# Pages of a paged cache fetched by GpSimd's row gathers instead of plain transfers, in a hybrid decoder step

## The chip, the cores and the metric

The kernel runs on one core of a Trainium2 chip. The engines are PE (TensorE, matrix products), DVE (VectorE), ACT (ScalarE), POOL (GpSimd) and SP (SyncE, which only issues transfers here). Each has its own queue, works it off in order, and waits for others by semaphores. The metric is the device time of one execution in microseconds (us), the median of several runs.

## The reference, cut to what matters

One step of two layers is computed for a prompt of 512 rows and for 8 samples with one new row each. The part that the change touches is the attention of the samples (NSA, native sparse attention), whose keys and values lie in paged caches in HBM: 128 rows a page, 8 pages a sample, and a page table that says which physical page each is.

```python
    s_c = jnp.einsum('btghd,bngd->btghn', qg, kc, preferred_element_type=f32)
...
    p_c = masked_softmax(s_c, m_c)
    o_c = jnp.einsum('btghn,bngd->btghd', p_c, vc.astype(f32))
...
    imp = jnp.einsum('btghn,nj->btgj', p_c, overlap_matrix(kc.shape[1], n_slc))
...
    _, idx = lax.top_k(score, topn)
...
    s_s = jnp.einsum('btghd,bgtnld->btghnl', qg, sel[..., 0, :], preferred_element_type=f32)
...
    o_s = jnp.einsum('btghnl,bgtnld->btghd', p_s, sel[..., 1, :].astype(f32))
...
    o = g[..., 0:1] * o_c + g[..., 1:2] * o_s + g[..., 2:3] * o_w
```

Here `kc`, `vc` are all rows of the compressed cache behind a small MLP, `sel` the 16 blocks of 64 rows that `imp` ranks highest, and `o_w` the same attention on a window of 512 rows.

With 1024 cached rows a sample has 16 whole blocks and its own new row, so nearly all pages of the selected cache are used, and the kernel loads them all and masks. There are three kinds of pages, 64 of each: of the compressed cache (`c_cmp`, 128 rows by 256 floats, 128 KB), of the selected keys (`c_sk`, 128 by 128, 64 KB) and of the selected values (`c_sv`, 64 KB). The window's keys and values (`c_wk`, `c_wv`) aren't paged.

## The kernel before, in words

Every dense product is made in three matmuls of split operands (`mm3`, L309 to L313), since a float32 is held as a high and a low part. Such a tile covers 128 output channels by 520 rows in two halves, x0 (256 columns) and x1 (264), 24 matmuls each.

The first stage (to about 285 us) makes q, k, v from the input (`wh_q`, `wh_k`, `wh_v`), rotates them, and runs the samples' compress and key products between those tiles, in the order of the list `ORDER` (L70): `q`, `k` are dense tiles, `c0` to `c7` are `compress(b)` of sample b, `r0` to `r5` are `scores_of`, `p` is a preparation, `d` the gates, `n` a normalisation. Behind the list come the 40 `xz` tiles (L990), whose matmuls the scheduler spreads to fill PE's idle time. They write one buffer `u`, whose last 11 columns POOL copies out (`sstg<-u`, L1002), then `uc`, then `uth`. Attention of the prompt follows, from about 285 to 690 us (`sc` the scores, L1110; `po` the value products, L1186; `ptl`, `pth` the split parts of its softmax; `QS` its scaled and split queries), with the xz tiles in its gaps. In it the samples' value products run too: 12 steps of `nsa_sample_out` (L1598) with a tile `vt` each, of which the first 8 take paged values. `st`, `Cb`, `Bm`, `xs`, `cum` are loads of the state-space part, which is prepared then.

`gather` (L804) fetches one page. SP reads its number out of the table `pti` ([1, 64], loaded at L741) into a register, and a plain transfer with an address that depends on it follows on SP (its lines stand in the diff below).

`compress(b)` (L923) fetches 8 pages into a tile `cc` and multiplies it in 32 matmuls (`cmpAB`, L934). `scores_of` (L1494) fetches 16 pages into a tile `kt` for r0 to r3 and makes the products `scS` (L1491); for r4 and r5 it takes `c_wk` in one plain transfer of 1 MB. `cc` and `kt` share three buffers (tag `big`), so that a gather waits until the tile that is three allocations earlier is used up. `vt` has two buffers. All weights (`raw_...`, L301) also come over SP's queue.

The Tile scheduler sets the order of every engine: it simulates a timeline with costs of its own and puts the instructions of each engine in the order that this gives. So an edit at one place can move instructions at many others.

Of the kernel before, what the change touches and what calls it, by code (L numbers as in the profile page):

```python
# [11 lines left out]
F32 = mybir.dt.float32  # L12
F32R = mybir.dt.float32r
I32 = mybir.dt.int32
BF16 = mybir.dt.bfloat16
AF = mybir.ActivationFunctionType
ALU = mybir.AluOpType
# [13 lines left out]
NPHYS = 80  # L31
# [226 lines left out]
def step_kernel(ctx: ExitStack, tc: tile.TileContext, I, O):  # L258
    nc = tc.nc
# [12 lines left out]
    def V(name, j=0):  # L272
        o, n = VEC[name]
        return vec[:, o + j:o + j + 1]
# [65 lines left out]
    def rstd(wk, ps, scale, name, last=None, out=None):  # L340
        n = ps.shape[-1]
        if last is not None:
            last = table(last)
        l = wk.tile([128, 266], F32, tag="lnv", name="lnv", bufs=1)
        r = wk.tile([128, 266], F32, tag="rs", name=name, bufs=2)[:, :n] if out is None else out
        with tc.issue_after(last.ins) if last is not None else ExitStack():
            nc.scalar.activation(l[:, :n], ps, AF.Ln, bias=epsT, scale=scale)
            done_["exp"] = nc.scalar.activation(r, l[:, :n], AF.Exp, scale=-0.5)
        return r
# [332 lines left out]
    def mixer(begin):  # L682
# [7 lines left out]
        def gen(n=512, name="gen"):  # L690
            return mp.tile([128, 512], F32, tag="g", name=name, bufs=3)[:, :n]
# [20 lines left out]
        ap = ax.enter_context(tc.tile_pool(name="ma", bufs=1))  # L712
# [4 lines left out]
        vcS = ap.tile([64, NB, 128], F32, name="vcS")  # L717
        vnew = ap.tile([64, 128], F32, name="vnew")
        pnT = ap.tile([64, 128], F32, name="pnT")
        pti = ap.tile([1, 64], I32, name="pti")  # L720
        u_ = ap.tile([128, T], F32, name="u")
        uc = ap.tile([128, T], F32, name="uc")
        hp = ap.tile([128, 24, NB], F32, name="shp")
# [6 lines left out]
        tp = p1.enter_context(tc.tile_pool(name="mt", bufs=2))  # L730
        x = []
        for hf in range(2):
            x.append(tp.tile([128, KD, 266], F32, tag="big", bufs=BIG, name="x"))
            n = HALF[hf][1] - X0[hf]
# [3 lines left out]
                wq = [wload(I["w_in"][0], 1, "k", "u")[0]]  # L738
        alr = tp.tile([128, 32], F32, name="alr", bufs=1)
        rsm = tp.tile([128, T], F32, name="rsm", bufs=1)  # L740
        nc.sync.dma_start(pti, I["pt"])  # L741
        c0_, c1_ = CST["cos"][0], CST["maskc"][0]
        cst = tp.tile([128, c1_ - c0_], F32, name="cst", bufs=1)

# [11 lines left out]
        def behind_x(hf, ins):  # L756

            with tc.issue_after(ins):
                if hf == 0:
                    nc.scalar.dma_start(cst, I["cst"][:, c0_:c1_])  # L760
                    nc.scalar.dma_start(vec[:, 64:], I["vec"][:, 64:])
                    return
                nc.scalar.dma_start(w2, I["w2"])
                nc.scalar.dma_start(alr, I["alr"].to_broadcast([128, 32]))
                nc.scalar.dma_start(b2v, I["b2v"].to_broadcast([64, 128]))
                nc.scalar.dma_start(pe.rearrange("p a b c -> p (a b c)"), I["pe"])
                for kv in range(2):
                    nc.scalar.dma_start(w1[kv].rearrange("p a b -> p (a b)"), I["w1"][kv])

        for hf, (c0, c1) in enumerate(HALF):  # L770
            ps = gen(c1 - c0, "ns")
            o, e = c0 - X0[hf], c1 - X0[hf]
            xh, xl = x_in[hf]
            for k in range(KD):
                sq = P["bk"].tile([128, 266], F32, tag="sq", name="sq", bufs=SQB)[:, :c1 - c0]
                last = nc.scalar.activation(sq, x[hf][:, k, o:e], AF.Square)
                if hf == 0 and k == 0:
                    behind_x(0, last.ins)
                nc.tensor.matmul(ps, ones, sq, start=k == 0, stop=k == KD - 1)
                if hf:  # L780
                    nc.vector.tensor_scalar(xh[:, k], x[hf][:, k, 0:e], V("ng", k), None, op0=ALU.mult)
                else:
                    nc.scalar.activation(xh[:, k], x[hf][:, k, 0:e], AF.Copy, scale=V("ng", k))
                nc.vector.scalar_tensor_tensor(xl[:, k], x[hf][:, k, 0:e], V("ng", k), xh[:, k].bitcast(F32), op0=ALU.mult,
                                               op1=ALU.subtract)
            rstd(P["bk"], ps, 1.0 / D, "rs1", None, rsm[:, c0:c1])
# [15 lines left out]
                split(xh[:, k], xl[:, k], xf)  # L802

        def gather(dst, src, n):  # L804

            page = nc.values_load(pti[0:1, n:n + 1], engines=(mybir.EngineType.SP,), min_val=0, max_val=NPHYS - 1,
                                  skip_runtime_bounds_check_because="the table holds numbers of the cache's pages")
            nc.sync.dma_start(dst, src.rearrange("(n p) c -> n p c", p=128)[bass.ds(page, 1)].rearrange("n p c -> p (n c)"))

        def dense2(mt, name):  # L810
            w = wq.pop() if wq else wload(I["w_in"][mt], 1, name, "u")[0]
# [66 lines left out]
        for kv in range(2):  # L878
# [25 lines left out]
            else:  # L904
                for g in range(2):
# [3 lines left out]
                                               op1=ALU.add)  # L909
# [13 lines left out]
        def compress(b):  # L923
            ccb = tp.tile([128, 8, 256], F32, tag="big", bufs=BIG, name="cc")
            for n in range(8):
                gather(ccb[:, n], I["c_cmp"], b * 8 + n)
            cv = ccb.rearrange("p n (v g j c) -> p v j g n c", v=2, g=2, j=8)
            for kv in range(2):
                hid = tp.tile([128, 2, 64], F32, tag="chs", name="chs", bufs=2)
                nc.vector.memset(hid[:, :, 63:64], 0.0)  # L930
                psa = gen(256, "cmpAB").rearrange("p (a g n) -> p a g n", a=2, g=2)
                for a in range(2):
                    for j in range(8):
                        nc.tensor.matmul(psa[:, a].rearrange("p g (n c) -> p g n c", c=8), w1[kv][:, a * 8 + j],  # L934
                                         cv[:, kv, j], start=j == 0, stop=j == 7)
                ub = tp.tile([128, 2, 64], F32, tag="ub", name="ub", bufs=2)
                nc.scalar.activation(ub, psa[:, 1], AF.Identity, bias=bias[:, kv:kv + 1])
                nc.vector.tensor_add(hid[:, :, 0:63], psa[:, 0, :, 0:63], ub[:, :, 1:64])
                th = tp.tile([128, 2, 64], F32, tag="cts", name="cts", bufs=2)
                nc.scalar.activation(th, hid, AF.Tanh, scale=0.5)  # L940
                nc.vector.scalar_tensor_tensor(hid, th, 1.0, hid, op0=ALU.add, op1=ALU.mult)
                ps = gen(128, "kvcS")
                if kv == 0:
                    nc.tensor.matmul(ps, w2[:, 0:128], hid.rearrange("p g c -> p (g c)"), start=True, stop=True)
                    for g in range(2):
                        sl = slice(g * 64, g * 64 + 64)
                        nc.scalar.activation(kcS[sl, b], ps[sl, g * 64:g * 64 + 64], AF.Identity,
                                             bias=V("cb2", 0)[sl], scale=0.5)
                else:
                    for g in range(2):  # L950
                        nc.tensor.matmul(ps[0:64, g * 64:g * 64 + 64], hid[:, g], w2[:, 128:192], start=True, stop=True)
                    nc.vector.scalar_tensor_tensor(vcS[:, b], ps[0:64], 0.5, b2v, op0=ALU.mult, op1=ALU.add)

        prep, scores_of, softmaxes = nsa_sample(mp, gen, C, tp, knew, qs, kcS, PT, pnT, gS, gather)
        dtg = tp.tile([128, T], F32, name="dtg", bufs=1)

# [5 lines left out]
        for op in ORDER.split():  # L962
            n = int(op[1:])
# [61 lines left out]
        for c in range(5):  # L1025
            n = 128 if c < 4 else NB
# [45 lines left out]
        tp = bp.enter_context(tc.tile_pool(name="mb", bufs=2))  # L1072
# [146 lines left out]
        def state_rows(tp, g, q=nc.sync):  # L1219
# [6 lines left out]
            for t in range(4):  # L1226
                for n in range(2):
# [7 lines left out]
                    yield  # L1235

        sample, sample_end = nsa_sample_out(gen, tp, first, PT, pnT, vcS, vnew, gather, d_yn)
        rows_of = itertools.chain(*(state_rows(tp, g, nc.gpsimd) for g in range(HG)))
        for hg in range(4):
# [15 lines left out]
        tp = sp_.enter_context(tc.tile_pool(name="ms", bufs=1))  # L1255
# [397 lines left out]
    with tc.tile_pool(name="wum", bufs=3, side="right") as P["wu"]:  # L1653
        new = mixer(begin)()
# [30 lines left out]
```

## Time and profile before

| | us |
|---|---|
| median of 3 runs (1977.76 to 1982.85) | 1979.02 |
| the profiled execution | 1979.54 |
| its span, first to last instruction | 1977.8 |
| PE busy | 1824.6 (92%) |
| DVE busy | 1427.8 (72%) |
| ACT busy | 969.3 (49%) |
| POOL busy | 181.6 (9%) |

The mean granted clock of PE is 0.964 of full speed. "Busy" of an engine leaves out the issuing of transfers on SP. A wait is put down to the producer that ended last. The chain of work that ended last holds PE for 67% of its length, DVE for 12% and transfers for 6%.

### The profile page before, as it was taken

To read this page: it belongs to the slowest core of one execution; us is meant where nothing else is said; L and a number is where in the kernel's file an instruction comes from. 1 tells how busy PE (TensorE), PEld (TensorE's weight loads), DVE (VectorE), ACT (ScalarE), POOL (GpSimd) and SP (SyncE) were. 2 spreads that over 40 slices of the span, in tenths; PEclk is the share of its full clock that TensorE was granted. 3 is DMA by queue.
4 is the path that set the end of the run, shared out by engine and by line. 5 is a ranking of instruction groups with operands and counts; after the bars stand their busy time and mean duration, and the time that the engine had idled before them with its cause. 6 is when DMAs were issued, how large, how long until landed. Compare 5 with 4: busy or idle time off the path is not lost.

```text
span 1977.8 us, 37956 instructions
## 1 busy us (share of the span) xinstructions
PE 1824.6 (92%) x14411; PEld 1706.2 (86%) x14411; DVE 1427.8 (72%) x3404; ACT 969.3 (49%) x2083; POOL 181.6 (9%) x226
## 2 busy tenths in 40 slices
PE   6998869899899889999899999997998989999997
PEld 5997868788788788988899999996766889999997
DVE  5764759788788698978767776575787765666766
ACT  3223436566467577656555433344126755444433
POOL 0000011010000003130000111000100000000100
PEclk9999989899899989999999999998998999999999
DMA  8446254253331385434245433221453223434421
GB/s 288 120 137 189 76 157 147 79 168 101 114 99 60 90 287 168 143 132 126 75 144 164 133 107 109 86 72 47 104 143 108 86 75 118 123 118 123 144 65 49
DMA packets 125947, 240.90 MB, mean 122 GB/s; under 512 B 16499, under 2 KB 63236, under 8 KB 125444
## 3 DMA queue, kind: packets, MB, share of 16 engines
q1 hardware_dynamic: 120676, 221.45, 36.6%
q0 software_dynamic: 4000, 13.73, 2.3%
q10 hardware_dynamic: 1088, 3.29, 0.4%
q8 instruction: 114, 1.87, 0.4%
q14 instruction: 69, 0.57, 0.1%
HBM read 200.75 MB, written 30.88 MB: 117 GB/s over the span
## 4 chain that ended last, share of the span: by engine, by line
PE 67%; DVE 12%; DMA 6%; ACT 6%; SPq 5%; issue 3%; POOL 1%; ACTq 0%; DVEq 0%; POOLq 0%
PE up L311 8%; PE up L312 8%; PE up L313 8%; PE acc L311 5%; PE acc L312 5%; PE acc L313 5%; PE dn L311 4%; PE dn L312 4%; PE dn L313 4%; SPq L607 3%; PE cmpAB L934 2%; PE pT L1173 1%; PE yd L1359 1%; PE po L1187 1%; DVE wl_xz L293 1%
## 5 line engine op out<-in xcount | busy, mean ns | idle before, releaser
L311 PE MATMUL dn<-gh,wh_dn 128*128 128x256 f32 (+1 forms) x704 | 198.0, 285 | 4.2 <-ACT gh L462 2.6
L313 PE MATMUL dn<-gh,wl_dn 128*128 128x256 f32 (+1 forms) x704 | 199.1, 284 | 0.0
L312 PE MATMUL dn<-gl,wh_dn 128*128 128x256 f32 (+1 forms) x704 | 198.8, 283 | 0.0
L450 DVE SCALAR_TENSOR_TENSOR c<-up,vec,c 128x511 f32<-128x511 f32 (+2 forms) x216 | 139.1, 646 | 14.6 <-ACT c L447 14.2
L311 PEld LDWEIGHTS dn<-gh,wh_dn 128*128 128x128 f32 x704 | 131.9, 189 | 5.6 <-ACT gh L462 2.9
L312 PEld LDWEIGHTS dn<-gl,wh_dn 128*128 128x128 f32 x704 | 133.4, 189 | 0.4 <-POOL gl L463 0.2
L313 PEld LDWEIGHTS dn<-gh,wl_dn 128*128 128x128 f32 x704 | 133.0, 189 | 0.0
L463 POOL TENSOR_TENSOR gl<-gm,gh 128x520 fp32r<-128x520 f32 (+2 forms) x54 | 61.8, 1144 | 703.5 <-ACT gh L462 703.4
L445 DVE TENSOR_TENSOR up<-up,rsx 128x520 f32<-128x520 f32 (+2 forms) x108 | 65.0, 604 | 81.3 <-PE up L313 79.8
L477 DVE TENSOR_TENSOR facc<-dn,facc 128x256 f32<-128x256 f32 (+1 forms) x160 | 66.4, 425 | 67.0 <-PE dn L313 66.6
L292 ACT ACTIVATE wh_up<-raw_up 128x1024 fp32r<-128x1024 f32 x68 | 72.0, 1059 | 72.7 <-PE up L312 47.2
L311 PE MATMUL acc<-x0hm,wh_xz 128*128 128x256 f32 x320 | 98.1, 307 | 6.0 <-ACT uc L999 3.7
L293 DVE TENSOR_TENSOR wl_up<-raw_up,wh_up 128x1024 fp32r<-128x1024 f32 x68 | 83.3, 1225 | 23.6 <-ACT wh_up L292 23.4
L312 PE MATMUL acc<-x0lm,wh_xz 128*128 128x256 f32 x320 | 95.1, 297 | 0.0
L313 PE MATMUL acc<-x0hm,wl_xz 128*128 128x256 f32 x320 | 94.9, 296 | 0.0
L311 PE MATMUL acc<-x1hm,wh_xz 128*128 128x264 f32 x320 | 93.4, 292 | 0.8 <-ACT u L997 0.8
L312 PE MATMUL acc<-x1lm,wh_xz 128*128 128x264 f32 x320 | 92.9, 290 | 0.0
L313 PE MATMUL acc<-x1hm,wl_xz 128*128 128x264 f32 x320 | 92.7, 290 | 0.0
L447 ACT ACTIVATE c<-up,vec 128x520 f32<-128x520 f32 (+2 forms) x108 | 74.8, 694 | 33.4 <-DVE up L445 32.7
L292 ACT ACTIVATE wh_dn<-raw_dn 128x1024 fp32r<-128x1024 f32 (+1 forms) x48 | 47.5, 989 | 88.2 <-PE dn L312 62.3
L293 DVE TENSOR_TENSOR ptl<-pT,pth 128x512 fp32r<-128x512 f32 (+1 forms) x96 | 65.1, 685 | 33.7 <-ACT pth L292 33.5
L292 ACT ACTIVATE pth<-pT 128x512 fp32r<-128x512 f32 (+1 forms) x96 | 56.3, 596 | 58.0 <-PE pT L1173 54.5
(583 smaller groups left out, 6857.4 us busy)
## 6 DMA issues: line engine op xcount, KB each, us to landing
raw_up<-in_w_up SPq DMA_DIRECT2D x68, 512.0 KB, 3.7
raw_xz<-in_w_in SPq DMA_DIRECT2D x40, 512.0 KB, 3.8
raw_dn<-in_w_down SPq DMA_DIRECT2D x32, 512.0 KB, 3.9
raw_wo<-in_w_out SPq DMA_DIRECT2D x24, 512.0 KB, 3.8
raw_pw<-in_w_pw SPq DMA_DIRECT2D x24, 512.0 KB, 4.0
spill<-uth SPq DMA_DIRECT2D x40, 260.0 KB, 2.5
st<-in_st SPq DMA_DIRECT2D x40, 256.0 KB, 3.0
cc<-in_c_cmp SPq DMA_DIRECT2D x64, 128.0 KB, 2.5
```

The lines of the kernel that those rows point to most:

```text
L292: nc.scalar.activation(hi, src, AF.Copy)
L293: (eng or nc.vector).tensor_sub(lo, src, hi.bitcast(F32))
L311: nc.tensor.matmul(ps, hi[:, wc], xh, start=first, stop=False)
L312: nc.tensor.matmul(ps, hi[:, wc], xl, start=False, stop=False)
L313: nc.tensor.matmul(ps, lo[:, wc], xh, start=False, stop=last)
L445: nc.vector.tensor_mul(u(a, e0), u(a, e0), rv[:, a:e0])
L447: nc.scalar.activation(c[:, rs], u(r0, r1), AF.Identity, bias=V("fb", l * 44 + mt), scale=W(2, mt))
L450: nc.vector.scalar_tensor_tensor(c[:, a:e], u(a - d, e - d), W(2 - d, mt), c[:, a:e], op0=ALU.mult, op1=ALU.add)
L463: nc.gpsimd.tensor_sub(gl[:, rs], gm[:, rs], gh[:, rs].bitcast(F32))
L477: nc.vector.tensor_add(f, ps, f)
L607: nc.sync.dma_start(x4[m][j * 32:j * 32 + 32, i, a:b], glu[m][i * 32:i * 32 + 32, 1 + j + a:1 + j + b])
L934: nc.tensor.matmul(psa[:, a].rearrange("p g (n c) -> p g n c", c=8), w1[kv][:, a * 8 + j], cv[:, kv, j], start=j == 0, stop=j == 7)
```

## The change

`gather` becomes one indirect transfer on POOL's queue: for each of the 128 partitions it fetches the row of the cache whose number stands in column n of a table `idx`, [128, 64]. To make that table, the page table is loaded into all 128 partitions (a broadcast transfer), an IOTA on POOL writes each partition's number, and two DVE operations compute page × 128 + partition. The reads of `pti` into SP's registers and the 192 transfers on SP are gone; `c_wk` and `c_wv` stay plain transfers on SP. The bytes and the buffers are the same. Lines behind L775 are 5 later in the changed kernel.

```diff
-        pti = ap.tile([1, 64], I32, name="pti")
+        idx = ap.tile([128, 64], I32, name="idx")
...
-        nc.sync.dma_start(pti, I["pt"])
+        pti = tp.tile([128, 64], I32, name="pti", bufs=1)
+        nc.sync.dma_start(pti, I["pt"][0:1, :].to_broadcast([128, 64]))
...
+        ptf = tp.tile([128, 2, 64], F32, tag="qz", name="ptf")
+        nc.gpsimd.iota(ptf[:, 0], pattern=[[0, 64]], base=0, channel_multiplier=1,
+                       allow_small_or_imprecise_dtypes=True)
+        nc.vector.tensor_copy(ptf[:, 1], pti)
+        nc.vector.scalar_tensor_tensor(idx, ptf[:, 1], 128.0, ptf[:, 0], op0=ALU.mult, op1=ALU.add)
...
         def gather(dst, src, n):
-
-            page = nc.values_load(pti[0:1, n:n + 1], engines=(mybir.EngineType.SP,), min_val=0, max_val=NPHYS - 1,
-                                  skip_runtime_bounds_check_because="the table holds numbers of the cache's pages")
-            nc.sync.dma_start(dst, src.rearrange("(n p) c -> n p c", p=128)[bass.ds(page, 1)].rearrange("n p c -> p (n c)"))
+            nc.gpsimd.indirect_dma_start(out=dst, out_offset=None, in_=src,
+                                         in_offset=bass.IndirectOffsetOnAxis(ap=idx[:, n:n + 1], axis=0))
```

The scheduler makes another order of this. On POOL, the place between the copies of old state at its start (`o_...`) and the first copy of u, before:

```order
L543 DMA o_ch<-in_h_cf 16x15360
L417 DMA o_fh<-in_h_ff 16x5632
L986 ISA
L986 TENSOR_TENSOR shist<-shist,vec 128x576
L1002 COPY sstg<-u 128x11 x5
L1085 MEMSET masks 128x384
```

and now:

```order
L417 DMA o_fh<-in_h_ff 16x5632
L812 DMA cc<-in_c_cmp,idx 128x256 x32
L812 DMA kt<-in_c_sk,idx 128x128 x32
L812 DMA cc<-in_c_cmp,idx 128x256 x8
L812 DMA kt<-in_c_sk,idx 128x128 x16
L812 DMA cc<-in_c_cmp,idx 128x256 x8
L812 DMA kt<-in_c_sk,idx 128x128 x16
L812 DMA cc<-in_c_cmp,idx 128x256 x16
L1007 COPY sstg<-u 128x11
L991 TENSOR_TENSOR shist<-shist,vec 128x576
L1007 COPY sstg<-u 128x11 x5
```

All 128 gathers of `cc` and `kt` stand there in one queue: c0 to c3, r0 and r1, c4, r2, c5, r3, c6 and c7.

On POOL in attention, behind the loads of the state (`st`, numbered by buffer), before:

```order
L1230 DMA st_6315<-in_st 128x512
L1230 DMA st_6321<-in_st 128x512
L1230 DMA st_6508<-in_st 128x512
L1230 DMA st_6514<-in_st 128x512
L1002 COPY sstg<-u 128x11 x6
L1224 DMA Cb<-d_bc 128x4x128 x2
L1230 DMA st_6520<-in_st 128x512
L1230 DMA st_6526<-in_st 128x512
```

and now:

```order
L1235 DMA st_5750<-in_st 128x512
L812 DMA vt<-in_c_sv,idx 128x128 x8
L1235 DMA st_5937<-in_st 128x512
L1007 COPY sstg<-u 128x11
L1235 DMA st_5943<-in_st 128x512
L1007 COPY sstg<-u 128x11
L812 DMA vt<-in_c_sv,idx 128x128 x8
L1007 COPY sstg<-u 128x11
L1229 DMA Cb<-d_bc 128x4x128 x2
```

The 64 gathers of `vt` now stand in groups of 8 between the copies of u and the state's loads.

On PE, at the first product of attention (`sc`); `rowsT` and `rowsS` are small transposes of the state-space part. Before:

```order
L311 MATMUL acc<-x1hm,wh_xz 128x264
L1057 MATMUL rowsT<-cst_77,col 32x128 x4
L1061 MATMUL rowsS<-cst_77,av 32x8 x2
L312 MATMUL acc<-x1lm,wh_xz 128x264
L313 MATMUL acc<-x1hm,wl_xz 128x264
L311 MATMUL acc<-x1hm,wh_xz 128x264
L312 MATMUL acc<-x1lm,wh_xz 128x264
L313 MATMUL acc<-x1hm,wl_xz 128x264
L1110 MATMUL sc<-KH_159,QS 128x32
L1111 MATMUL sc<-KL_161,QS 128x32
```

and now:

```order
L313 MATMUL acc<-x1hm,wl_xz 128x264
L1062 MATMUL rowsT<-cst_77,col 32x128 x4
L1066 MATMUL rowsS<-cst_77,av 32x8 x2
L311 MATMUL acc<-x1hm,wh_xz 128x264
L312 MATMUL acc<-x1lm,wh_xz 128x264
...
L311 MATMUL acc<-x1hm,wh_xz 128x264
L312 MATMUL acc<-x1lm,wh_xz 128x264
L313 MATMUL acc<-x1hm,wl_xz 128x264
L1115 MATMUL sc<-KH_159,QS 128x32
L1116 MATMUL sc<-KL_161,QS 128x32
```

Five xz matmuls stood between rowsS and the first `sc`, and now there are 66. Counted from the start of the program, 1418 matmuls stood ahead of the first `sc`, and now 1659; the 241 more are xz matmuls. The first matmul of c7 has 1075 matmuls ahead of it before and 1187 now. Behind the first `sc` there are 1440 xz matmuls before and 1199 now.

## Rows read from the trace of the kernel before

**Rows 1.** The page's busy line: engine, us, share of span, instructions.

```profile
PE 1824.6 (92%) x14411; PEld 1706.2 (86%) x14411; DVE 1427.8 (72%) x3404; ACT 969.3 (49%) x2083; POOL 181.6 (9%) x226
```

**Rows 2.** Stretches: busy us (instructions) of PE, PEld, DVE, ACT, POOL; granted clock; DMA share; GB/s.

```profile
150.00:285.00 135.00, 105.60 (x809) 95.95 (x808) 82.13 (x231) 53.06 (x126) 9.93 (x18) 0.91 0.43 135
285.00:690.00 405.00, 375.32 (x2760) 331.88 (x2758) 324.96 (x1028) 249.72 (x613) 26.08 (x45) 0.96 0.36 110
```

**Rows 3.** Waits of PE, 140 to 285 us: for whom, us, times, longest.

```profile
PE sc L1110 <- DVE QS L1104: 8.1, 1, 8.1
PE acc L1014 <- DVE uth L1010: 7.2, 1, 7.2
PE scS L1491 <- DMA kt<-in_c_wk: 4.4, 2, 3.5
PE scS L1491 <- DMA kt<-in_c_sk: 2.8, 2, 1.6
PE acc L311 <- ACT uc L999: 2.1, 1, 2.1
PE imp L1537 <- DVE pcT L1535: 1.7, 1, 1.7
PE cmpAB L934 <- DVE vnew L871: 1.4, 1, 1.4
PE impg L1541 <- DVE im L1539: 1.0, 1, 1.0
```

**Rows 4.** Waits of PE, 285 to 690 us: three of them.

```profile
PE po L1187 <- DVE ptl L293: 8.3, 7, 2.8
PE po L1186 <- ACT pth L292: 5.3, 6, 1.5
...
PE acc L311 <- ACT u L997: 3.1, 5, 1.7
```

**Rows 5.** SP: a run of gathers (start, us, how many), then its waits.

```profile
93.33 8.31 SPq L808 DMA_DIRECT2D kt<-in_c_sk  x10
...
154.99 6.30 SPq L808 DMA_DIRECT2D cc<-in_c_cmp  x8
...
SPq L808 <- PE cmpAB L934: 20.0, 4, 6.7
...
SPq L808 <- PE osum L1617: 12.9, 5, 3.5
...
SPq L806 <- DMA pti<-in_pt: 8.7, 1, 8.7
```

**Rows 6.** PE in order of time (start, us): a half tile, then c0, c1, c7.

```profile
55.84 0.28 PE L311 MATMUL acc<-x0hm,wh_q 128*128 128x256 f32 x1
...
58.33 0.28 PE L311 MATMUL acc<-x1hm,wh_q 128*128 128x264 f32 x1
...
61.83 3.73 PE L934 MATMUL cmpAB<-cc,w 128*128 128x128 f32 x32
...
89.57 3.74 PE L934 MATMUL cmpAB<-cc,w 128*128 128x128 f32 x32
...
205.75 3.84 PE L934 MATMUL cmpAB<-cc,w 128*128 128x128 f32 x32
```

**Rows 7.** A small DVE copy: total us, mean ns.

```profile
L917 DVE COPY qs<-qr 128x8 f32<-128x8 f32 x8 | 1.3, 163 | 0.0
```

**Rows 8.** POOL: the copy of u and plain transfers (durations in ns).

```profile
L1002 POOL COPY sstg<-u x24: 192/448/987, 220.3 to 642.0; 128x11 f32<-128x11 f32 x24
...
L1230 POOL DMA_DIRECT2D st<-in_st x24: 537/538/609, 270.7 to 541.9; - x24
...
L1224 POOL DMA_DIRECT2D Cb<-d_bc x6 | 4.5, 757 | 28.3 <-DMA d_bc<-bst 28.3
```

**Rows 9.** DMA issues: how many, KB each, median us to landing.

```profile
cc<-in_c_cmp SPq DMA_DIRECT2D x64, 128.0 KB, 2.5
...
chist<-in_h_cf POOLq DMA_DIRECT2D x8, 120.0 KB, 2.3
```


## Prediction

> **What bounds the kernel now.** I read the page's busy line first: TensorE (PE) is busy 1824.6 us of a span of 1977.8 [rows 1]. So time can be won or lost only where PE idles, and the stretches show where. In 150 to 285 us PE is busy 105.60 of 135.00 us, at a granted clock of 0.91; in 285 to 690 (attention) 375.32 of 405.00, at 0.96 [rows 2]. The idle time is 29.4 and 29.7 us. From 690 us on nothing of the changed code runs.
>
> The waits of PE in the first stretch come next [rows 3]. Two are long and are latencies of chains on other engines: 8.1 us for QS before the first attention product and 7.2 us for uth. The pages cost PE little: 2.8 us for kt, and 1.4 us which the view puts down to vnew, although it precedes a compress, so that I count it as a late cc page. Another 4.4 us is the window load of 1 MB, which stays a plain transfer. In attention the waits are many and short, and the longest are for the softmax parts ptl (8.3 us) and pth (5.3 us) [rows 4]: there the scheduler fills with whatever xz matmuls are left.
>
> Last, SP: a run of gathers issues ten in 8.31 us, 0.83 us each [rows 5]. SP also stood 20.0 us with a gather for a compress to free its buffer, with the weight loads behind it [rows 5]; but PE's waits name no weight load, so that time is off its path.
>
> **Removed.** The SP gathers with their table reads, 192 at 0.83 us, are off the path but for the 2.8 + 1.4 us of PE's waits: **−4.2 us**, provided that the pages now come in time.
>
> **Moved: PE's order.** Up to about c4 the two orders are the same. Later 241 xz matmuls that stood behind the first attention product stand ahead of it (the last piece of order shown with the change). A half tile of matmuls starts 21 of them between 55.84 and 58.33 us, 0.12 us each [rows 6], so 241 are 29 us. They can cover the waits for QS and uth, 8.1 + 7.2 = 15.3 us. I take **−14**, not all of it, because each of these tiles brings its own ACT and DVE work to the chain that QS hangs on. The short waits (uc, imp, impg, 4.8 us together) I leave, with the window load. The low end fills them also. The clock of 0.91 should rise with a denser PE; I count nothing for it, and 2 us at the low end.
>
> **Given back in attention.** There were 1440 xz matmuls at or behind the first attention product, and now some 1200, 17% fewer, to fill with. 17% of 29.7 us is **+5**.
>
> **Added: idx.** One IOTA, one cast and one multiply-add, on 128x64 values. The nearest small DVE copy takes 163 ns [rows 7], so these are 0.4 us on DVE, early, and the first gather isn't needed before c0's first matmul at 61.83 us [rows 6]. In before SP waited 8.7 us for the table, in front of the first gather [rows 5]; now the first of DVE's two operations waits for it, and the ropes of k stand behind that on DVE. The table's transfer is now 128 rows of 256 bytes and no longer one, but stands at the same place in SP's queue. Nothing for it; if DVE stood 3 us longer, that would cost up to 3.
>
> **Added: POOL's price p for one gather.** Before has no indirect transfer. Its plain POOL transfers of 128 rows hold POOL 538 ns (st, median) and 757 ns (Cb, mean) [rows 8], and land as SP's do: 120 KB from POOL in 2.3 us, 128 KB from SP in 2.5 [rows 9]. So landing changes nothing, and the low bound is 0.54 us. The high bound is a 1.1 us gather that is also held off by DVE as the little copy of u is: it takes 192 ns when free and 987 ns at most [rows 8], 0.8 us more, so 1.9. I take 1.1 to 1.2, twice the plain one, because each row's address must first be made from idx.
>
> What p decides is the **supply**. r0 takes the buffer of c1, which is used up at 89.57 + 3.74 = 93.3 us [rows 6]. From there 96 gathers follow in POOL's order (16 each for r0 to r3, 8 each for c4 to c7) until c7 has its data. c7's first matmul was at 205.75 us [rows 6]. 112 more matmuls now stand ahead of it (+13.4 us), and between 4.2 and 8.6 us of waits fall away, so that the need is at 210.6 to 214.5. With 2 us for landing the break-even pitch is (208.6 − 93.3)/96 = 1.20 to (212.5 − 93.3)/96 = 1.24 us. Above it PE runs at POOL's pace: 96 × (p − 1.22). I followed the 12 batches through the three buffers in this way, too: no stall from pages up to 1.1, +1.7 us at 1.2, +11 at 1.3, +27 at 1.5, +49 at 1.75, +74 at 2.0. I count **+1**.
>
> **Sum** against the profiled execution's 1979.5 us (0.5 over the median of 1979.02, with 1.7 us of it outside the span): −4.2 − 14 + 5 + 1 = −12.2, so **1967 us**.
>
> **The rivals.** *POOL as the bound* (the other side): one queue with one gather behind another, and a p above the break-even. Without the page term the sum is 1966.3; at p = 1.33 its 13 us are eaten up and the kernel is as slow as before; at 1.5 it takes 1993, at 2.0 2040. For it: POOL has to make 128 addresses for each, while on SP one plain instruction took 0.83 us with its table read. Against it: POOL has little else to do here, busy 9.93 of 135 us [rows 2], and SP was no faster than 0.83, with PE waiting only 4.2 us for pages.
>
> *DVE holds POOL off*: the copy of u was held off by up to 0.8 us [rows 8]. If every gather met this, p would be 1.9, which gives 96 × 0.68 = 65 us, some 2032. DVE is busy 82.13 of 135 us in that stretch [rows 2]. Against it: in attention, where DVE is busier (324.96 of 405), the 24 st transfers took 537 ns at least and 609 at most [rows 8], so the issue of a plain one was not held off at all. The Trainium skill ("SBUF — State Buffer", "Who interferes with whom") has this rule: while VectorE runs an operation that takes the shared port pair, GpSimd can't write its transfer descriptors, and 620 ns become some 3100. By those figures a gather might take some 3.1 us, and the estimate would be 96 × 1.88 = 180 us more, about 2147. These st rows don't agree, since none took over 0.61 us; a gather, which must also read idx from SBUF, no row shows.
>
> *The gain is given back*: the first attention product comes after the chain c7, gates, QS, and later work is bound by chains and not by fillers. Then the 14 us only move into attention. Also, the 64 vt gathers now stand on POOL between the copies of u, and ACT can't write the next u before its copy: a vt gather that waits for its buffer (PE, osum; SP stood 12.9 us for that [rows 5]) holds ACT's next u, and so PE. The result: some 1979.5 − 4.2 + 2 = 1977. For it: PE's waits for u and uc in attention are 3.1 us already [rows 4]. Against it: DVE and ACT have idle time there, and xz tiles remain to the end of it.
>
> That the change doesn't do what it says is not open: all 192 gathers stand on POOL.
>
> **How the numbers follow.** The forecast, with p up to 1.25: 0.42. Given back: 0.12. POOL as the bound with p from 1.25 to 1.40, 1973 to 1985 us: 0.10; with p above 1.40: 0.28. DVE holds POOL off: 0.08. A difference under 0.3% (5.9 us, 1973.1 to 1985.0) is about what can't be told from no change here. So faster 0.42, same 0.12 + 0.10 = 0.22, slower 0.28 + 0.08 = 0.36. The low end is 1967 less the short waits (4.8), the rest of the 15.3 (1.3), the clock (2) and the page term (1), some 1957. The high end is p = 1.75, 1966 + 49 = 2015. Left out are the held-off case, p beyond 1.75 (0.07) and a time below 1957 (0.04), 0.19 in all. Cases of both signs are likely; the forecast's own range is 1957 to 1974.
>
> **What would show it.** The mean distance between POOL's indirect transfers in a run of 16 is p. If the forecast holds, it is under 1.25 us, c7's first matmul comes near 211 us or a little later, PE's waits in 150 to 285 lose uth and QS, and PE idles about 5 us more in attention. If POOL bounds, PE waits for kt at r1, r2 and r3 and for cc at c4 and c5, each a few us, and the stretch up to the first attention product grows. If DVE holds it off, single gathers scatter from p to several times p. If the gain is given back, PE's waits for u and for softmax parts grow by what QS and uth lose. The forecast is wrong if p is above 1.33, whatever the order gains.

## The result: 0.9% slower, and the profile of the changed kernel

| | us |
|---|---|
| before, median of 4 runs beside it | 1978.39 (1977.38 to 1982.85) |
| changed, median of 4 runs | **1996.61** (1993.76 to 1998.97) |
| ratio | 1.0092, 95% interval 1.0071 to 1.0113 |
| the profiled execution of the changed kernel, its span | 1996.18, 1994.4 |

The forecast was 1967 us, faster. The kernel became 18 us slower, inside the range of 1957 to 2015 but with the other sign. First the busy line of the page and the two stretches of the changed kernel, with the columns of [rows 1, 2]:

```profile
PE 1837.0 (92%) x14411; PEld 1710.9 (86%) x14411; DVE 1427.6 (72%) x3406; ACT 976.7 (49%) x2087; POOL 379.9 (19%) x419
...
150.00:285.00 135.00, 114.21 (x842) 101.05 (x841) 78.05 (x200) 51.84 (x114) 55.98 (x57) 0.91 0.35 110
285.00:690.00 405.00, 373.53 (x2691) 328.54 (x2690) 324.38 (x1044) 247.74 (x615) 97.61 (x119) 0.94 0.37 116
```

POOL's busy time doubles from 181.6 us [rows 1] to 379.9: that is the 192 gathers. In 150 to 285 us PE is busier than in [rows 2] (114.21 against 105.60 us), as the moved matmuls promised. In 285 to 690 it is as busy as before, but at a granted clock of 0.94 where [rows 2] has 0.96. Two later traces of the same order (d and e below) have 0.95 and 0.96 there, so this difference alone says little.

POOL's queue in order of time (start, us, then what it waited for ahead of it), and the tile view of the compress pages (duration in ns: least, median, most; first and last start):

```profile
137.60 0.95 POOL L812 DMA_INDIRECT cc<-in_c_cmp,idx  x1 [0.30 <-issue]
138.85 1.77 POOL L812 DMA_INDIRECT cc<-in_c_cmp,idx  x1 [0.30 <-issue]
140.92 0.95 POOL L812 DMA_INDIRECT cc<-in_c_cmp,idx  x1 [0.30 <-issue]
...
L812 POOL DMA_INDIRECT cc<-in_c_cmp,idx x64: 942/946/1963, 25.2 to 215.4; - x64
...
DMA to landing us min/median/max: 2.7/3.3/7.0
```

A gather holds POOL 0.95 us and 0.30 us pass before the next, so the free pitch is 1.25 us. Some are held longer, here up to 1.96 us: all 41 of the 192 that took over 1.1 us began while DVE ran an instruction, and the 51 that began with DVE idle took 1.03 us at most. Over the 96 gathers from 88.85 to 215.41 us the mean pitch is (215.41 − 88.85)/95 = **1.33 us**, 7.8 us in all above the free pitch, and the holding is the whole of that. A page lands 3.3 us after its issue, where a plain one took 2.5 [rows 9].

The waits of PE from 140 to 310 us (for whom, us, times, longest), to be read beside [rows 3]:

```profile
PE pTs L1592 <- DVE pk L1576: 5.6, 1, 5.6
PE scS L1496 <- DMA kt<-in_c_wk: 4.4, 1, 4.4
PE kvcS L949 <- DVE chs L946: 3.6, 1, 3.6
PE sc L1115 <- DMA raw_xz<-in_w_in: 3.5, 1, 3.5
PE pcT L1539 <- DVE pc L1536: 3.5, 1, 3.5
PE cmpAB L939 <- DMA cc<-in_c_cmp,idx: 2.8, 1, 2.8
...
PE acc L1019 <- DVE uth L1015: 0.6, 1, 0.6
```

The wait for uth, 7.2 us in [rows 3], is gone but for 0.6. The wait for QS is not: it is the 3.5 us that the view puts down to raw_xz, in place of 8.1. The first of DVE's four QS ends at 306.97 us, and sc starts 0.2 us behind it, as it did before (275.24 and 275.45):

```profile
306.55 1.77 DVE L1109 TENSOR_TENSOR QS<-qh,QS 64x256 fp32r<-64x256 f32 x4 [0.83 <-ACT QS L1108]
307.17 0.25 PE L1115 MATMUL sc<-KH,QS 128*128 128x32 f32 x1 [3.52 <-DMA raw_xz<-in_w_in]
```

In place of what was won stand pTs, kvcS and pcT, which wait for DVE's work on the compressed keys and on the samples' scores (`chs`, `pc`, `pk`), on the way to the first attention product: 12.7 us. For pTs and pcT the reason is in PE's order: the new order took the fillers (xz matmuls that PE can run while a chain is under way) away from there. Before, 72 xz matmuls stood directly ahead of pTs and 24 ahead of pcT; now 30 and none do. The pages cost PE 2.8 us (c4). And in attention, beside [rows 4], the wait for ptl has grown from 8.3 to 12.7 us:

```profile
PE po L1192 <- DVE ptl L293: 12.7, 15, 3.2
```

What the forecast had left out is the part behind attention. The waits of PE from 690 to 1640 us, first of the kernel before:

```profile
PE ns L332 <- DVE sq L328: 17.4, 8, 4.6
...
PE up L311 <- ACT sq L326: 6.6, 2, 3.5
PE up L311 <- DVE c L450: 3.8, 2, 2.8
```

and of the changed kernel:

```profile
PE ns L332 <- DVE sq L328: 21.5, 9, 5.0
PE up L311 <- DVE c L450: 14.5, 5, 4.8
```

No line that was edited runs there, and yet the up products of the two ConvFFNs wait 14.5 us for DVE's convolution (`c`) in place of 3.8, while their 6.6 us for ACT's `sq` are gone. The order of the instructions differs there too.

### The profile page after: what moved, and what is told of

Same layout as the page of the kernel before. It is cut to its first block, busy times and chain, and to the rows that moved or that the text cites. A ratio compares the mean times of both kernels' runs of the same rounds, so it can differ in the third digit from the quotient of the medians.

```text
span 1994.4 us, 37420 instructions
## 1 busy us (share of the span) xinstructions
PE 1837.0 (92%) x14411; PEld 1710.9 (86%) x14411; DVE 1427.6 (72%) x3406; ACT 976.7 (49%) x2087; POOL 379.9 (19%) x419
## 4 chain that ended last, share of the span: by engine, by line
PE 41%; DVE 6%; ACT 3%; DMA 2%; SPq 2%; issue 2%; POOL 0%; DVEq 0%; ACTq 0%; POOLq 0%
PE up L311 8%; PE up L312 8%; PE up L313 8%; PE dn L311 4%; PE dn L312 4%; PE dn L313 4%; SPq L607 2%; DVE facc L629 1%; PE pw L311 1%; PE pw L312 1%; PE pw L313 1%; DMA raw_pw<-in_w_pw 1%; PE dn L622 1%; DVE xf L384 1%; DVE sq L328 1%
```

## The experiments

**The means.** The order of PE, DVE and ACT can be held: a table at the end of the file lists, for each of the three engines, the order that another build has, and an edge without a semaphore goes between each two neighbours. POOL and SP stay with the scheduler. The two new index operations on DVE are left out of the table. So the transfers and the order can be changed apart. The edit, on either kernel (the tables differ):

```diff
-        step_kernel(tc, I, O)
+        step_kernel(tc, I, O); pin(nc, tc, SKIP)
...
+def pin(nc, tc, skip):
...
+    dep = mybir.DependencyInfo(mybir.DependencyClass.NoSync, mybir.DependencyReason.DATA)
+    for e, text in PIN.items():
...
+        for a, b in zip(order, order[1:]):
+            tc.add_manual_dep(mine[b], mine[a].name, dep, reason="pin")
```

**1. Transfers and order apart.** Three kernels on one chip (chip 7). The gathers, held to the order of before:

> The changed kernel, but PE, DVE and ACT are held to the order in which their instructions stand in the kernel before (a table of places at the end of the file, one edge from each instruction to the next on its engine, no wait added). The gathers stay on POOL. Theory 'order': the new order on PE, DVE and ACT costs the time, and POOL's row gathers, at 1.25 us each, cost next to nothing; then this is within 0.5% of before, 1970 to 1988. Theory 'pace': POOL's queue is what costs; c7 stands 112 matmuls earlier in this order, so that its data are due at about 200 us and 96 gathers from 93 us on allow 1.09 us each; at 1.25 us PE waits some 15 us more for pages, so 1990 to 1998.

Measured: 2097.48 us (2080 to 2104), ratio 1.0599 (1.0563 to 1.0635). The plain transfers, held to the changed order:

> The kernel before with its plain transfers on SP, but PE, DVE and ACT are held to the order in which their instructions stand in the changed kernel. Theory 'order': about as slow as the changed kernel, 1990 to 2000. Theory 'pace': the order is harmless or better, and pages come at 0.83 us each, so 1965 to 1982.

Measured: 1986.17 us, ratio 1.0044 (1.0028 to 1.0059), between the two theories. The changed order held, and each gather split into two of half the row:

```diff
-            nc.gpsimd.indirect_dma_start(out=dst, out_offset=None, in_=src,
-                                         in_offset=bass.IndirectOffsetOnAxis(ap=idx[:, n:n + 1], axis=0))
+            w = src.shape[1] // 2
+            for h in range(2):
+                nc.gpsimd.indirect_dma_start(out=dst[:, h * w:h * w + w], out_offset=None, in_=src, element_offset=h * w, in_offset=bass.IndirectOffsetOnAxis(ap=idx[:, n:n + 1], axis=0))
```

> The changed kernel held to its own order on PE, DVE and ACT, but each gather is made as two, each of 128 rows of half the length, so that POOL's queue has 384 of them. What the supply sum says: if the price is one per instruction, the pitch of a page is 2.5 us, and the 96 gathers up to c7 cost 96 x (2.5 - 1.24) = 121 us, so about 2115; if it went with the bytes, it would be about 2000. Theory 'order' and theory 'pace' both expect the first; they differ in what they say of 1.25 us. Only if PE's waits for pages don't grow by some 100 us is the supply sum itself wrong.

Measured: 2334.76 us. POOL's queue of this kernel shows the price of a half-length gather:

```profile
60.68 0.95 POOL L814 DMA_INDIRECT cc<-in_c_cmp,idx  x1 [0.31 <-issue]
61.94 0.94 POOL L814 DMA_INDIRECT cc<-in_c_cmp,idx  x1 [0.30 <-issue]
```

Half the bytes take the same 0.95 + 0.30 us: the price is one of the instruction, not of the length. The number of rows was 128 in both, and no run varied it; and c's time says nothing of the price, since the stops told of next are in it. Of the order, b says that it costs some 8 us with no gather in the program. But a and c gave times that no theory had: 2097 where both orders with their own transfers take under 2000. Their waits of PE (a, 30 to 300 us; "issue" is time in which PE waited for nothing that the trace shows):

```profile
PE cmpAB L939 <- issue: 31.5, 33, 2.4
PE acc L312 <- issue: 10.4, 11, 1.7
```

I call these **stops**. There are none in the changed kernel's trace. They had to be cleared up first, since they hide the 18 us.

**2. Is it the holding?** The changed kernel again, and the changed kernel held to its own order, on chip 1:

> The changed kernel as it is, once more, on the chip and beside the runs of this job. In the two held kernels with gathers PE was stopped in steps of about 0.70 us, with no wait that the trace names, in stretches that begin some 11 us after a row of gathers starts and end a few us after its last; the changed kernel's trace had none of that, although its POOL queue and its first 840 matmuls are the same as in the kernel held to the order of before. Theory 'order': the stops come from how the instructions stand or are held, so this is again near 1996.6 (1990 to 2003) and has none. Theory 'chip': they come from the chip or from how a program lies in memory on it, so this has them too and takes 2050 to 2110.

> The changed kernel, with PE, DVE and ACT held to the order that they have in it anyway, so that every engine's order is the same; only the holding edges are new, and they are no waits. If the stops come from the holding (theory 'hold'), this has them, and takes 2050 to 2110. If holding does nothing, it is the changed kernel again: 1990 to 2003, or whatever that takes in this job.

Measured: 1996.89 us (ratio 1.0116, 1.0083 to 1.0148) and 1998.34 us (1.0113, 1.0081 to 1.0146), neither with a stop. The result repeats on a second chip, and holding an order costs nothing.

**3. Early order and late order apart.** The program was cut at the first ConvFFN: ahead of it the changed order, behind it that of before. f has the gathers, g the plain transfers, h the changed order throughout with only the vt pages gathered and cc and kt by plain transfers, and a2 is kernel a again (all on chip 4). f and g are the edit shown first, with the tables joined at that place; h adds to the held changed kernel:

```diff
         def gather(dst, src, n):
+            if src is not I["c_sv"]:
+                with tc.issue_after(LAST[0]) if LAST else ExitStack():
+                    page = nc.values_load(pti[0:1, n:n + 1], engines=(mybir.EngineType.SP,), min_val=0, max_val=NPHYS - 1,
...
+                    LAST[:] = [nc.sync.dma_start(dst, src.rearrange("(n p) c -> n p c", p=128)[bass.ds(page, 1)].rearrange("n p c -> p (n c)")).ins]
+                return
```

> The changed kernel, held on PE, DVE and ACT to its own order up to the first ConvFFN (traced instructions before the first up-projection) and from there to the order of the kernel before. No code of that late part is touched by the change. In the two traces the plain kernel in the changed order loses some 3 us against before between the end of attention and the first up tile of the ConvFFN (976.1 to 979.1, after gaining 2), and another 3.4 us up to the second one. Theory 'late order': these some 8 us are the price of another order in untouched code, so this takes 1997 - 8 = 1989 (1984 to 1993). Theory 'not the order' (clock, or the time at which that part starts): 1994 to 2000.

> The kernel before with plain transfers, held to the changed kernel's order up to the first ConvFFN and to its own order behind that. Theory 'late order': 1986.2 - 8 = 1978, or a little under before, since the changed order had gained 2 us at the end of attention: 1974 to 1981. Theory 'not the order': 1984 to 1988 as before.

> The changed kernel held to its own order, but only vt's 64 pages are row gathers on POOL; the pages of cc and kt are plain transfers on SP again. The plain kernel in this order took 1986.2 and the changed kernel 1997, so the gathers cost some 10.5 us. By the traces half of it lies ahead of the first product of attention (pages of cc and kt) and half inside attention (vt, or the clock). Theory 'POOL is late with cc and kt': this takes 1986 to 1988, with the first sc at 302 as with plain transfers. Theory 'vt delays attention': 1991 to 1994.

> The gathers in the order of before, once more, beside two kernels with gathers in the changed order on one chip. If the stops of PE in steps of 0.70 us belong to this program, it takes 2080 to 2105 again and the other two have no stops. If they belonged to the chip of that job, this takes some 1990, or the others have them too.

Measured: f 2096.11 us (ratio 1.0606) with stops; g **1975.36** (0.9999, 0.9981 to 1.0017); h 2036.24 (1.0285); a2 2102.36, with stops again. f and h lie far outside what was expected of them. From g against b follows that the order of the late part, where nothing was edited, is what the changed order costs: with the late order of before, its ratio falls from 1.0044 to 0.9999. Of h little can be used: its chained plain transfers on SP hold the weight loads up (one wait of PE for x0hm is 17.4 us), and it has stops only behind 315 us, where its gathers begin.

f has the changed kernel's order on PE, DVE and ACT up to the first ConvFFN, and yet it stops there. PE in order of time in f, then POOL at the same time:

```profile
120.74 0.37 PE L313 MATMUL acc<-x0hm,wl_q 128*128 128x256 f32 x1 [1.51 <-issue]
...
122.16 0.37 PE L313 MATMUL acc<-x0hm,wl_q 128*128 128x256 f32 x1 [0.62 <-issue]
...
120.03 0.95 POOL L812 DMA_INDIRECT kt<-in_c_sk,idx  x1 [0.30 <-issue]
```

and f in a stretch of such stops (us; PE, PEld, DVE, ACT, POOL; granted clock, DMA share, GB/s):

```profile
182.00:204.00 22.00, 6.86 (x23) 4.80 (x21) 1.59 (x2) 1.06 (x1) 15.09 (x15) 0.57 0.27 84
```

PE gets 23 matmuls done in 22 us. POOL's gathers keep their usual 0.94 to 0.95 us.

**4. Chip or program?** The changed kernel, the same held to its order, and f, on chip 3:

> The changed kernel once more, on the same chip as the two runs beside it; its PE stops (steps of some 0.7 us for which the trace shows no wait, at rows of gathers) are what is looked for. Theory chip: the stops go with the chip, so either all three kernels of this job have them (this one then near 2095 to 2105 us) or none (this one 1997 us). Theory program: the stops go with the program; this one has none and takes 1994 to 2001 us whichever chip it is.

> The changed kernel held to its own order by edges without semaphores. Theory chip: as the run before it, about 2100 us with stops or 1998 us without. Theory program: none, 1994 to 2001 us.

> Gathers, the changed order up to the first ConvFFN, the order of before behind it (2096 us with stops on the chip where it ran). Theory chip: as the two runs ahead of it in this job; without stops it takes the changed kernel's time less the 9 us of the late order, about 1986 us. Theory program: 2085 to 2110 us with stops, on a chip where the two others have none.

Measured, one run each: 1992.76, 1998.03 and **1980.49** us, no stop in any. Kernel f, unchanged, had taken 2084.7 to 2109.8 us in six runs on chip 4. So the stops go with the chip, or with its state at the time, not with the program.

**5. The split, on a chip without stops** (chip 12): the changed kernel, kernel a, kernel f and kernel g side by side:

> The changed kernel on the chip of the three runs beside it. Theory chip: where the run of the gathers in the order of before (2097 us so far, on two chips) shows stops of PE, this one shows them too and takes 2090 to 2110 us; where that one shows none, this one takes 1993 to 2000 us. Theory program: 1993 to 2000 us in any case.

> Gathers, with PE, DVE and ACT held to the order of before. Theory chip: 2090 to 2105 us on a chip whose changed kernel stops too; on a chip without stops the price of the gathers in the old order alone, 1984 to 1990 us (the 5 to 11 us that they cost in the changed order). Theory program: about 2097 us with stops on any chip.

> Gathers, changed order up to the first ConvFFN, order of before behind it. On a chip without stops: 1980 to 1987 us (one look gave 1980.5), that is the changed kernel's time less the 9 to 12 us of the late order. On a chip with stops: 2085 to 2110 us. Theory program has no place for both having been seen.

> The plain transfers in the orders of the run before it: 1973 to 1978 us on any chip. The run before it less this one is the price of the gathers alone with the order held equal: 5 to 11 us without stops by the theory that POOL's pace and the single transfers behind it cost that, under 3 us if all that the change loses is the order, 110 to 130 us with stops.

| | us | ratio to before (1977.12) |
|---|---|---|
| o: plain, changed order early, late order of before | 1976.94 | 0.9990 (0.9974 to 1.0005) |
| n: the same with gathers | 1986.28 | 1.0040 (1.0025 to 1.0055) |
| l: the changed kernel (one run) | 1997.97 | |
| m: gathers, the order of before throughout | 2027.40 | 1.0249 (1.0224 to 1.0274) |

Kernel a, 2097 us on chip 7, takes 2027 here: the theory of the chip holds once more. The gathers alone cost n − o = **9.3 us**; the late order l − n = **11.7 us** (10.6 with the median of d on the other chip); the early order o − before = −0.2 (by the interval −5.1 to +1.0), so no gain that the runs can tell. m missed its expectation, 1984 to 1990.

Where the 9.3 us lie is read from n and o, whose orders are equal. Waits of PE, 130 to 310 us, in o:

```profile
PE scS L1491 <- DMA kt<-in_c_wk: 8.6, 2, 8.2
PE pTs L1587 <- DVE pk L1571: 5.6, 1, 5.6
PE pcT L1534 <- DVE pc L1531: 3.5, 1, 3.5
...
PE kvcS L944 <- DVE chs L941: 1.4, 1, 1.4
```

and in n:

```profile
PE scS L1496 <- DMA kt<-in_c_wk: 4.0, 1, 4.0
...
PE kvcS L949 <- DVE chs L946: 3.6, 1, 3.6
...
PE scS L1496 <- DMA kt<-in_c_sk,idx: 3.1, 3, 2.2
PE cmpAB L939 <- DMA cc<-in_c_cmp,idx: 2.6, 1, 2.6
```

The pages come late by 3.1 + 2.6 us and kvcS waits 2.2 us more, while the window load that shares the buffer waits 4.6 less: 3.3 us in all. From the first product of the samples' scores to the gates' product n takes 120.0 us and o 114.7. Attention, from its first product to its last, takes 383.9 us in n and 377.9 in o. The stretch 310 to 680 us, o above n (columns as before):

```profile
310.00:680.00 370.00, 342.32 (x2503) 296.86 (x2501) 309.92 (x1005) 235.33 (x585) 23.96 (x43) 0.97 0.36 113
...
310.00:680.00 370.00, 342.96 (x2493) 300.95 (x2493) 308.85 (x1015) 234.35 (x589) 93.74 (x111) 0.95 0.37 117
```

PE idles 27.7 us in the one and 27.0 in the other. What differs is the granted clock, 0.97 and 0.95, and 0.02 of 370 us is 7 us, as an estimate. The other traces go the same way. From its first product to the start of its last, attention takes 382.6 to 386.3 us in the nine with gathers and the new early order, at a granted clock of 0.938 to 0.960, and 377.9 to 379.8 us in the three with plain transfers (b, g and o), at 0.964 to 0.968; PE idles 28 to 31 us in all of them. I can't say which small change in PE's idle time moves the clock there.

Why the gathers cost 50 us in the old order (m) and 9 in the changed one is seen on POOL. In m the 16 gathers of the first vt pages stand ahead of the state scan's loads (start, us):

```profile
307.89 0.95 POOL L812 DMA_INDIRECT vt<-in_c_sv,idx  x1 [0.30 <-issue]
...
313.07 0.62 POOL L1221 DMA_DIRECT2D cum<-d_rows  x1
...
321.12 0.34 DVE L1383 TENSOR_TENSOR smp<-xs,cum 64x8 f32<-64x8 f32 x2 [21.87 <-DMA cum<-d_rows]
...
324.30 0.69 DVE L1015 SCALAR_TENSOR_TENSOR uth<-uth,u 128x520 f32<-128x520 f32 x1
```

DVE, held to the old order, stands 21.87 us for `cum`; uth is behind that on DVE, ACT's next u waits for uth, and PE waits 15.1 us for u:

```profile
PE po L1192 <- DVE ptl L293: 17.3, 8, 7.9
PE acc L311 <- ACT u L1002: 16.2, 3, 15.1
```

In the kernel before, and in the changed one, the same load stands here:

```profile
272.83 0.58 POOL L1216 DMA_DIRECT2D cum<-d_rows  x1
```

```profile
327.54 0.61 POOL L1221 DMA_DIRECT2D cum<-d_rows  x1
```

It is 55 us later in the changed kernel as well, behind the same 16 gathers, but there DVE's order has the state scan later, and PE's the moved matmuls ahead: DVE takes `smp` at 339.11 us without a wait. The other part of what m loses are its pages. One wait of a compress product, 8.0 us, has no releaser in the view; but the last gather of its page (c6) is issued at 203.94 us and lands at 206.55, and the product starts then:

```profile
203.94 0.95 POOL L812 DMA_INDIRECT cc<-in_c_cmp,idx  x1 [0.30 <-issue]
206.96 5.74 PE L939 MATMUL cmpAB<-cc,w 128*128 128x128 f32 x32 [8.02 <-issue]
```

With 9.6 us for kt and 2.9 for cc, which the view names, PE waits 20.5 us for pages in m, against 4.2 before. That is what theory 'pace' had said of kernel a, some 15 us more. m comes to its first sc 17.5 us late (292.98 against 275.45 us) and loses the rest in attention (438.5 against 408.9 us). So with the gathers in place the changed early order is worth 41 us (2027.4 − 1986.3) over that of before.

**6. The changed kernel on a chip with stops.**

> The changed kernel once more, on whichever chip is met. If it is one of the two on which other kernels with gathers had stops of PE: 2090 to 2110 us if the stops go with the chip, 1993 to 2000 us if the changed kernel's own program escapes them. On another chip 1993 to 2000 us by either.

Measured: 2003.76 us (one run, with before at 1979.58 beside it), 3.8 above the upper end, and no stop; but it was chip 0, not 4 or 7. So this stays open.

## Why the forecast was wrong, step by step

- **"From 690 us on nothing of the changed code runs."** True of the code, and the step that failed most. The scheduler orders the whole program anew, so that the ConvFFN was reordered as well. From the start of attention's last product to the end the changed kernel takes 1300.9 us against 1293.4 before, b (no gathers) 1301.9; g, o and n, with the late order of before, 1291.5, 1294.4 and 1290.3. All eight traces with the changed late order lie at 1300.9 to 1306.8, the six with that of before at 1288.5 to 1294.4. PE waits 13.8 us for the convolution and 21.4 for ns in l, 3.5 and 16.4 in n, with the same transfers on the same chip; in exchange n waits 7.4 us for `sq`, and l does not. The runs price it at 9 to 12 us, by n against l and by g against b. The price was counted at 0. One thing that differs there is ACT: it loads its function tables (ACT_TABLE_LOAD, 1.28 us each) 29 times in the kernels with the changed late order and 25 times in those with that of before, and the four more lie behind 690 us. At the first ConvFFN two of these loads stand ahead of a `c` that DVE waits for, and PE's up product (2.16 us) behind DVE. First l (ACT, then DVE), then the same `c` in n, where it stands ahead of them:

```profile
963.23 1.28 ACT L347 ACT_TABLE_LOAD   x1
...
965.03 1.28 ACT L348 ACT_TABLE_LOAD   x1
...
966.65 0.55 ACT L447 ACTIVATE c<-up,vec 128x256 f32<-128x256 f32 x1
...
967.23 1.00 DVE L450 SCALAR_TENSOR_TENSOR c<-up,vec,c 128x255 f32<-128x255 f32 x2 [4.20 <-ACT c L447]
...
959.18 0.56 ACT L447 ACTIVATE c<-up,vec 128x256 f32<-128x256 f32 x1
```

  How much of the 9 to 12 us these loads make, no run shows; nor what POOL and SP add, whose order was left to the scheduler.
- **Moved, −14, and given back, +5.** The wait for uth went and that for QS became shorter, as the mechanism said: the 15.3 us are 3.7 in o, where there is no gather. But there PE waits on the same stretch for pTs 5.6 and pcT 3.5 us, and 8.6 for c_wk, which was 4.4 [rows 3]: 13.3 us more. The short waits mostly go. All in all PE's idle time from the start of the span to the first sc falls from 46.2 to 40.6 us: 5.6 us were won there, and 14 were counted. In attention nothing was given back: between its first and last product PE idles 27.8 us in o and 27.1 before. The profiled execution of o has a lead of 3.9 us at the last product of attention (680.5 against 684.4 us) and of 2.9 at the end, and the medians show none (−0.2 us). In sum −9 was predicted and about 0 came. The rival "the gain is given back" had the amount nearly right and the place wrong: most of it is given back at once, ahead of the first attention product. The counts of matmuls behind this step were off, their differences not: 1786 stood ahead of the first sc and 2027 do now (not 1418 and 1659), 241 more as taken; 1632 xz matmuls stood behind it and 1392 do now, 15% fewer and not 17, which makes the +5 some +4.
- **POOL's price p, 1.1 to 1.2.** Measured: 1.25 free, 1.33 in the mean, the value at which the forecast had the kernel as slow as before. A gather by itself is cheaper than was taken, 0.95 us, but 0.30 us pass between two, which no row of before showed. By the replay 1.33 should have stalled PE for pages by 11 us or more. It did by 3.2 (5.7 in n), because the other half of that step was wrong as well: c7 was not needed at 211 us but at 227.30. With plain transfers (b) c7 starts at 223.76 us, so this is the order's doing for the most part. The 112 more matmuls are right, but PE is busy 196.7 us up to c7 in b against 180.4 before, 16 more and not 13.4; and none of the 4.2 to 8.6 us of waits fell away, since PE idles 16.0 us between its first matmul and c7 against 14.3. (The upper need is 205.75 + 13.4 − 4.2 = 214.95 us, not 214.5, which makes the upper break-even 1.25.)
- **Removed, −4.2.** The waits for cc and kt were 2.8 + 1.4 us and are 3.2 (the changed kernel, 0.4 of it for kt) to 5.7 (n) now. Nothing was won. The three steps on the transfers, −4.2 and +1 and idx at 0, made −3.2; with equal orders they are +9.3, of which some 5 us lie ahead of the gates and 6 in attention by the profiled executions (behind attention these differ by 4 us the other way, with equal orders: that is the scatter between two executions).
- **idx at nothing.** The first gather waits until 25.18 us for it, but the first compress starts at 57.1 us (before: 61.83). Right.
- **DVE holds POOL off.** Right in kind and small in size. Over the nine traces with gathers and the new early order, 334 of 1728 gathers took over 1.1 us, and all of these began while DVE was busy; the 470 that began with DVE idle took 1.04 us at most. In five of these traces (d, i, k, n and p) one vt gather took 3.9 to 4.1 us, beside eight operations of DVE without a gap. In n:

```profile
386.39 4.08 POOL L812 DMA_INDIRECT vt<-in_c_sv,idx  x1 [0.30 <-issue]
...
386.20 3.24 DVE L1172 TENSOR_SCALAR pt<-pt,mx 128x512 f32<-128x512 f32 x8
```

  But most gathers are hardly held (median 0.946 us, mean 1.09 for cc), and the holding is 0.1 us in the mean, not the 0.68 of this rival. The Trainium skill ("SBUF — State Buffer", "A bandwidth-pool intuition that's wrong (but worth ruling out)") has a transfer that GpSimd describes take some 3100 ns in place of 620 beside a copy on VectorE. Those five gathers agree with that in size, and the mean does not.
- **The copies of u behind the vt gathers.** This mechanism was named, with a price of 2 us. In the changed kernel ACT waits 1.8 us for such a copy. But the loads of the state scan stand in the same queue, and m shows what they can cost (DVE's 21.87 us). I had not listed them.

The sum that the runs give: early order 0, gathers +9, late order +9 to +12, together 18 to 21 against the 18.2 measured. The forecast had −9, −3 and 0.

## What to carry to other kernels

Where a scheduler places the whole program, an edit early in it can reorder the late part too: compare the orders to the end, and to learn what an edit is worth hold the order of one build under the transfers of the other. Row gathers on POOL are priced per instruction, 1.25 us here whatever the row's length, so plain transfers in the same queue come later by 1.25 us for each gather ahead of them; list all that stands behind them, and not only the consumers of the pages. A filler that is moved to one wait can bare another: here 11.6 us were won at QS and uth, and 9.1 of them came back at pTs and pcT, from where the fillers had been taken. So count, ahead of every long chain, the fillers that stand there before and after.

## What was not expected of the hardware

- On two of the six chips known by number (4 and 7), PE stopped in steps of about 0.7 us while gathers ran and for a few us behind them, with no wait in the trace: kernel f 2096 us on chip 4, 1980.5 and 1986.3 us on chips 3 and 12; kernel a 2097 and 2102 on chips 7 and 4, 2027 on chip 12. Plain kernels on the same chips show none (b and g). In these traces the gathers themselves are not slower, and the instruction fetches take the same share of the DMA engines' time as in n (0.4 and 0.1%). The cause stays open, and so does whether the changed kernel as it is would stop there: it ran on chips 0, 1, 3 and 12 and, in the first runs, on one that isn't known, and never stopped.
- An indirect gather of 128 rows took 0.945 us with rows of 256 to 1024 bytes, and 0.30 us passed between two of them.
- In the nine traces counted above, a gather was held only when DVE was busy as it began, mostly by some tenths of a microsecond and at most to 4.1 us.
